# Small TensorE products of a decoder layer's mixing part: one weight shape and whole groups

## The chip, the cores and the metric

The kernel is one program on one core of a Trainium2 chip. The number that counts is the device time of one execution in microseconds (us); the median of three runs is compared. One further execution was recorded by the profiler, and all rows below are read from that one.

Each engine of the core works through its own instructions in order: TensorE (PE) multiplies, VectorE (DVE), ScalarE (ACT) and GpSimd (POOL) do the rest, and SyncE (SP) issues most transfers. An instruction waits for semaphores that other engines raise, and what stands behind it on its engine waits with it.

## What is computed

The reference is one inference step of one layer for 512 prompt positions and 8 samples, in float32. Cut to what matters:

```
x += 0.5 * SwiGLU_1(rms(x))
z  = rms(x) @ w_in                       # one projection, 8448 columns
y_A = RWKV-7 mixing of z's r | k | v | decay | iclr | gate columns
        S = S * decay - (S kk) b^T + v k^T ;  y = S r      # per head, 64 x 64 state
y_B = B * conv3(C * u)
x += (sigmoid(g_A) * y_A + sigmoid(g_B) * y_B) @ w_out
x += 0.5 * SwiGLU_2(rms(x)) ;  x += per-layer embedding ;  final norm
```

The change lies in the mixing part, from `z` to `y_A`.

## The kernel before

All activations stand transposed, 128 features by 520 columns (512 prompt positions and 8 samples), and products run over two halves of 260 columns. A big product of float32 accuracy is made of three passes (high part by high, low by high, high by low), each with 128x128 weights and 260 columns.

In the mixing part (`mix`) two kinds of work share TensorE. The **big products** are the projection's blocks (`product`, lines 792 to 794, 3120 passes in all; `big` in the rows). The **small products** belong to the recurrence. Sixteen heads are handled as eight pairs `p`, two heads on 128 partitions. Time is cut into 16 chunks of 32 positions. For each pair, `stage` prepares decays, keys and masks (its products are `dec`, `icl`, `kn`, `sc`, `bon`), `invert` inverts a triangular 32x32 matrix for each chunk (`ft`), `scan` carries the state through the 16 chunks for two pairs at once (`e` = 0 and 1), and `fin` normalises (`yt`, `gu`).

A chunk of `scan` is made of four groups of four float32 products. In the profile each of these products is two passes, so a group is "x8".

- State product (line 1155, called S below): `AR` by the state S, 64x64 weights, into the bank `xy`, whose rows 0..31 of each head become `u` and whose rows 32..63 become `y`.
- `u` product (line 1160, called W): the inverted matrix by the known rows of `UV`, 32x32 weights. Then two copies on DVE bring `u` into `UV` (line 1163).
- y product of the chunk before (line 1140, called Y): 64 rows by 32 columns of weights, into the other `xy` bank, and then ACT copies y out.
- State update (line 1172, `ds`): 64x64 weights, into the bank `us`. Two DVE operations make the next state (line 1175), one for each pair.

So W and Y use 32 columns of the array's width where S and `ds` use 64.

The functions are generators. A loop at the end of `mix` takes a step of one of them at a time by a planner's clock: a step yields the TensorE time that it is taken to cost and the delay until its generator may go on. That gives the order in which the program is traced. A scheduler then orders the instructions of each engine by readiness in its own model and by that trace order, so that two products of one group can be parted by big ones.

Two PSUM banks (`mw`) serve all small products of `stage`, `invert` and `fin`.

Of the kernel before, what the change touches and what calls it, by code (L numbers as in the profile page):

```python
# [8 lines left out]
F32 = mybir.dt.float32  # L9
# [720 lines left out]
def mix(tc, nc, mp, pp, dp, low0, wprep, mwps, mmps, V, VV, I, O, HS, YM, ysplit, wo_part, ident, pmask):  # L730
# [7 lines left out]
    nc.sync.dma_start(sft, I["sft"])  # L738
    nc.sync.dma_start(cst8, I["cv0"])
    nc.sync.dma_start(smask, I["smask"])  # L740
    nsh = mp.tile([P, NZ, B + 1], F32, name="nsh")
    omm = mp.tile([P, NZ], F32, name="omm")
    hka = mp.tile([P, 4, NT], F32, name="hka")
# [191 lines left out]
    def stage(p):  # L935
# [39 lines left out]

        if p % 2 == 0:
            both[p // 2] = [wide(n, [NC, 2, 64]) for n in ("AR", "UV")]
        ar, uv = both[p // 2]
        AR, UV = ar[:, :, p % 2, :].rearrange("p c (s t) -> p c s t", s=2), uv[:, :, p % 2, :]
        W = wide("W", [NC, 128], 4)  # L980
# [1 line left out]
        v1.tensor_copy(lam, eL[:, :, C])  # L982
        v1.tensor_tensor(AR[:, :, 1, :], c3(r[:, :T]), eL[:, :, 1:], ALU.mult)
        kk = kn
        for cs in GROUPS:
            ps = mwps("kn")
            for g in range(cs.start, cs.stop, GT):
                i = g // GT
                for h, hp in enumerate(HP):
                    nc.tensor.matmul(ps[hp, g - cs.start:g - cs.start + GT], rhs=ident[:GT, :GT], start=True, stop=True,  # L990
                                     lhsT=rs[:GT, 2 * i + h:2 * i + h + 1].broadcast_to([GT, 64]))
            v1.scalar_tensor_tensor(kk[:, cs], k[:, cs], V("k_k", p), ps[:, :cs.stop - cs.start], ALU.mult, ALU.mult)
            yield 0.2 * (cs.stop - cs.start) / GT, 0.5
        v1.scalar_tensor_tensor(AR[:, :, 0, :], c3(kk[:, :T]), -1.0, eL[:, :, 0:C], ALU.mult, ALU.mult)
        yield 0.0, 1.5
        v1.scalar_tensor_tensor(a, a, 1.0, kk, ALU.add, ALU.mult)
# [2 lines left out]
        v1.tensor_tensor(ei, c3(km[:, :T]), ei, ALU.mult)  # L999
        yield 0.0, 1.0  # L1000

        for c0 in range(0, NC, 8):
            ps = mwps("sc")
            for c in range(c0, c0 + 8):
                o = (c - c0) * 64
                for hp in HP:
                    nc.tensor.matmul(ps[hp, o:o + 64], lhsT=fl(BK[hp, c]), rhs=ar[hp, c, p % 2, :], start=True, stop=True)
            v1.tensor_tensor(W[:, c0:c0 + 8, 0:64], ps.rearrange("p (c x) -> p c x", x=64),
                             pmask[:, 0:64].unsqueeze(1).broadcast_to([P, 8, 64]), ALU.mult)
            yield 1.4, 0.6  # L1010

        dm = dp.tile([2, NC, C, CH], F32, tag="dm", name="dm", bufs=2)
        for h in range(2):
# [11 lines left out]
        rk = parts(rk, *t2("rk", N, ("kn", "a")))  # L1025
        yield 0.0, 2.5
        bon = tt("bon", 4)
        for cs in HALF:
            ps = small((blkr,), rk, cs, "bon")
            v1.tensor_tensor(bon[:, cs], vv[:, cs], ps, ALU.mult)  # L1030
            yield 0.25, 0.5
        pool.tensor_copy(bonS[:, p, :], bon[:, T:])

        v3 = c3(vv[:, :T])
# [12 lines left out]
    Nz = mp.tile([P, NC, C], F32, name="Nz")  # L1047
    pool.memset(F4, 0.0)
    pool.memset(Nz, 0.0)
    CH = C // 2  # L1050
    UP = (slice(0, C), slice(64, 64 + C))

# [3 lines left out]
    def invert(p):  # L1056
# [35 lines left out]
        for c0 in range(0, NC, 8):  # L1092
            ps = mwps("ft")
            for i in range(4):
                for odd in range(2):
                    for up in UP:
                        c = c0 + 2 * i + odd
                        qd = slice(up.start + C * odd, up.stop + C * odd)

                        nc.tensor.matmul(ps[qd, i * 128:i * 128 + 96], lhsT=W[up, c, 0:C], rhs=W[up, c, C:],  # L1100
                                         start=i == 0, stop=False, skip_group_check=True)
                        nc.tensor.matmul(ps[qd, i * 128 + 96:(i + 1) * 128], lhsT=Nz[up, c, :], rhs=W[up, c, 0:C],
                                         start=False, stop=False, skip_group_check=True)
            banks.append(ps)
            yield 1.0, 0.8
        for c0, ps in zip(range(0, NC, 8), banks):
            GM = mp.tile([P, 4, 128], F32, tag="Mr", name="GM")
            act.activation(fl(GM), ps, AF.Identity)
# [13 lines left out]

    def scan(q):

        AR, UV = both[q]
        W, lam, _ = zip(st_out[2 * q], st_out[2 * q + 1])
        Y = AR
        S, prev = mp.tile([P, 2, 64], F32, tag="S", name="S", bufs=3), None
        pool.memset(S, 0.0)

        def at(ps, rows, e):
            return ps[rows, 64 * e:64 * e + 64]

        def cols(ps, rows):
            return ps[rows, 0:128].rearrange("p (e x) -> p e x", e=2)

        def y_part(c, xy):
            for e in range(2):
                for hp in HP:
                    nc.tensor.matmul(at(xy, slice(hp.start + C, hp.stop), e), lhsT=W[e][hp, c, C:64],  # L1140
                                     rhs=UV[hp, c, e, :], start=False, stop=True, skip_group_check=True)

        def y_out(c, xy):
            if c % 2 == 0:
# [4 lines left out]

        for c in range(NC):  # L1150
            xy = pp.tile([P, 512], F32, tag="xy", name="xy", bufs=2)
            for e in range(2):

                for hp in HP:
                    nc.tensor.matmul(at(xy, hp, e), lhsT=AR[hp, c, e, :], rhs=S[hp, e, :], start=e == 0, stop=False,  # L1155
                                     skip_group_check=True)
            for e in range(2):
                for h in range(2):
                    up, kp = slice(64 * h, 64 * h + C), slice(64 * h + C, 64 * h + 64)
                    nc.tensor.matmul(at(xy, up, e), lhsT=W[e][kp, c, 0:C], rhs=UV[kp, c, e, :], start=False, stop=True,  # L1160
                                     skip_group_check=True)
            for up in (slice(0, C), slice(64, 64 + C)):
                v1.tensor_copy(UV[up, c], cols(xy, up))
            if c:
                y_part(c - 1, prev)
                y_out(c - 1, prev)
            prev = xy
            yield 0.76, 0.8
            ds = pp.tile([P, 512], F32, tag="us", name="ds")
            for e in range(2):  # L1170
                for hp in HP:
                    nc.tensor.matmul(at(ds, hp, e), lhsT=W[e][hp, c, 64:], rhs=UV[hp, c, e, :], start=True, stop=True)  # L1172
            S1 = mp.tile([P, 2, 64], F32, tag="S", name="S", bufs=3)
            for e in range(2):
                v1.scalar_tensor_tensor(S1[:, e, :], S[:, e, :], lam[e][:, c:c + 1], at(ds, slice(0, P), e),
                                        ALU.mult, ALU.add)
            S = S1
            yield 0.32, 0.8
        y_part(NC - 1, prev)
        y_out(NC - 1, prev)  # L1180
        nc.sync.dma_start(O["wkvp"][2 * q:2 * q + 2].rearrange("q p v -> p q v"), S)
        yield 0.2, 0.5

    def fin(p):
# [30 lines left out]
        act.activation(y1, ps, AF.Identity, scale=V("gn_w", p), bias=V("gn_b", p))  # L1215
        pool.tensor_tensor(y1, y1, bon[:, :T], ALU.add)
        yield 1.4, 2.3
        for j, cs in enumerate(HALF):
            ps = small(gup, sgd, cs, "gu")
            ts = slice(cs.start, min(cs.stop, T))  # L1220
            v1.scalar_tensor_tensor(y1[:, ts], y1[:, ts], 0.5, ps[:, :ts.stop - ts.start], ALU.mult, ALU.mult)
            if j == 1:
                act.activation(gS[:, p, :], ps[:, T - cs.start:], AF.Identity, scale=0.5)
            yield 0.33, 0.5
        y1s[p] = y1

    def sample():
# [239 lines left out]
```

## Time and profile before

| What | Value |
|---|---|
| Median of 3 runs | 1582.39 us (1580.38 to 1582.6) |
| The profiled execution | 1582.78 us, of which the span from the first to the last instruction is 1581.0 us |
| TensorE's mean granted clock | 0.967 of full |
| PE busy | 1513.4 us (96%) |
| DVE, ACT, POOL busy | 1082.8 us (68%), 769.4 us (49%), 396.4 us (25%) |
| Mixing part | from about 406 us to about 1108 us of the span |

Busy shares are averages over stages. A pass of TensorE overlaps the next, so the distance from the start of one row to the start of the next tells its price, and the length of a row does not.

### The profile page before, as it was taken

The page shows a single profiled execution, that of the slowest core. Times are in us where ns is not written, and L with a number is a line of the kernel's source. Part 1 is how long each engine was busy: PE and PEld are TensorE (multiplying, and loading weights), DVE is VectorE, ACT ScalarE, POOL GpSimd, SP SyncE. Part 2 cuts the span into 40 slices and gives each one's busy share as a digit, 9 for nine tenths or more (in the row PEclk, how much of TensorE's full clock was granted, in tenths as well). Part 3 has the DMA queues.
Part 4 walks back from the last instruction along what each step waited for, and adds up shares of the span by engine and source line. Part 5 has one row for each costly group of instructions (what it writes and reads, how often), then busy time and mean ns, then how long its engine had stood idle before and what let it go on. Part 6 is the DMA issues. An engine that isn't in the chain of part 4 may idle for free.

```text
span 1581.0 us, 36116 instructions
## 1 busy us (share of the span) xinstructions
PE 1513.4 (96%) x14772; PEld 1421.5 (90%) x14772; DVE 1082.8 (68%) x2347; ACT 769.4 (49%) x1352; POOL 396.4 (25%) x446
## 2 busy tenths in 40 slices
PE   8899999999999999999999999999989999999996
PEld 7799999998899988888888787799988999999996
DVE  8876666655797776568778357765688656666566
ACT  7655555555544424424442253143465555555543
POOL 0333433342322120111212004211004343434401
PEclk9899999999999999999999599899999999999998
DMA  5678888885332211212221122224336787888723
GB/s 179 160 164 183 181 179 185 177 202 137 98 85 79 84 38 53 65 43 65 75 71 44 37 74 77 88 78 149 96 93 168 177 182 182 180 187 177 168 60 112
DMA packets 116133, 191.08 MB, mean 121 GB/s; under 512 B 41800, under 2 KB 51016, under 8 KB 115968
## 3 DMA queue, kind: packets, MB, share of 16 engines
q1 hardware_dynamic: 92352, 138.44, 28.2%
q0 software_dynamic: 23616, 50.34, 19.8%
q8 instruction: 116, 1.90, 0.5%
q14 instruction: 49, 0.40, 0.1%
HBM read 177.73 MB, written 10.74 MB: 119 GB/s over the span
## 4 chain that ended last, share of the span: by engine, by line
PE 47%; DVE 8%; ACT 1%; DMA 1%; issue 1%; SPq 0%; DVEq 0%; ACTq 0%
PE big L171 9%; PE big L173 8%; PE big L172 8%; PE big L792 5%; PE big L794 4%; PE big L793 4%; PE ds L1172 2%; PE xy L1155 1%; DVE lo L132 1%; PE xy L1140 1%; PE xy L1160 1%; DVE raw L166 0%; DMA sdr<-stg 0%; DVE ft L1079 0%; DVE F L1081 0%
## 5 line engine op out<-in xcount | busy, mean ns | idle before, releaser
L130 ACT ACTIVATE hi<-raw 128x512 fp32r<-128x512 f32 (+2 forms) x427 | 318.4, 749 | 316.1 <-PE big L172 166.9
L792 PE MATMUL big<-xh,hi 128*128 128x260 f32 x1040 | 317.3, 305 | 0.4 <-DVE cc L862 0.2
L793 PE MATMUL big<-xl,hi 128*128 128x260 f32 x1040 | 306.2, 295 | 0.0
L794 PE MATMUL big<-xh,lo 128*128 128x260 f32 x1040 | 305.6, 294 | 0.5 <-DVE lo L132 0.5
L132 DVE TENSOR_TENSOR lo<-raw,hi 128x512 fp32r<-128x512 f32 (+2 forms) x263 | 239.2, 912 | 61.7 <-ACT hi L130 57.2
L792 PEld LDWEIGHTS big<-xh,hi 128*128 128x128 f32 x1040 | 202.2, 194 | 14.0 <-issue 0.5
L793 PEld LDWEIGHTS big<-xl,hi 128*128 128x128 f32 x1040 | 202.6, 195 | 5.3 <-issue 0.7
L171 PE MATMUL big<-hh,hi 128*128 128x260 f32 x704 | 203.5, 289 | 3.9 <-DVE x L470 3.9
L794 PEld LDWEIGHTS big<-xh,lo 128*128 128x128 f32 x1040 | 202.0, 194 | 5.4 <-DVE lo L132 0.8
L173 PE MATMUL big<-hh,lo 128*128 128x260 f32 x704 | 199.5, 283 | 0.0
L172 PE MATMUL big<-hl,hi 128*128 128x260 f32 x704 | 199.4, 283 | 0.0
L171 PE MATMUL big<-th,hi 128*128 128x260 f32 x640 | 182.8, 286 | 9.2 <-ACT th L319 5.3
L172 PE MATMUL big<-tl,hi 128*128 128x260 f32 x640 | 182.3, 285 | 3.6 <-DVE tl L320 3.6
L173 PE MATMUL big<-th,lo 128*128 128x260 f32 x640 | 181.2, 283 | 0.0
L171 PEld LDWEIGHTS big<-hh,hi 128*128 128x128 f32 x704 | 133.2, 189 | 7.7 <-DVE x L470 4.3
L470 DVE SCALAR_TENSOR_TENSOR x<-big,x 128x260 f32<-128x260 f32 x176 | 74.7, 426 | 94.8 <-PE big L173 94.8
L172 PEld LDWEIGHTS big<-hl,hi 128*128 128x128 f32 x704 | 133.3, 189 | 0.0
L173 PEld LDWEIGHTS big<-hh,lo 128*128 128x128 f32 x704 | 133.3, 189 | 0.0
L171 PEld LDWEIGHTS big<-th,hi 128*128 128x128 f32 x640 | 121.3, 190 | 11.0 <-ACT th L319 6.0
L172 PEld LDWEIGHTS big<-tl,hi 128*128 128x128 f32 x640 | 121.1, 189 | 4.9 <-DVE tl L320 4.9
L171 PE MATMUL big<-xh,hi 128*128 128x260 f32 x400 | 115.2, 292 | 7.9 <-ACT hi L130 5.4
L166 DVE TENSOR_TENSOR raw<-raw 128x512 f32<-128x512 f32 x160 | 114.0, 713 | 11.0 <-DMA raw<-in_wu 5.6
(306 smaller groups left out, 3488.2 us busy)
## 6 DMA issues: line engine op xcount, KB each, us to landing
raw<-in_win SPq DMA_DIRECT2D x66, 512.0 KB, 3.8
raw<-in_wd SPq DMA_DIRECT2D x80, 256.0 KB, 2.9
lo<-in_wd POOLq DMA_DIRECT2D x72, 256.0 KB, 4.6
raw<-in_wu SPq DMA_DIRECT2D x24, 512.0 KB, 3.7
raw<-in_wg SPq DMA_DIRECT2D x23, 512.0 KB, 4.4
raw<-in_wg SPq DMA_DIRECT2D x40, 256.0 KB, 3.5
raw<-in_wu SPq DMA_DIRECT2D x40, 256.0 KB, 3.7
lo<-in_wg POOLq DMA_DIRECT2D x18, 512.0 KB, 5.5
```

Source lines behind the costliest of these rows:

```text
L130: nc.scalar.activation(self.hi[:, ks], self.raw[:, ks], AF.Identity)
L132: self.eng.tensor_tensor(self.lo[:, ks], self.raw[:, ks], self.hi[:, ks].bitcast(F32), ALU.subtract)
L166: nc.vector.tensor_tensor(self.raw, a.raw, b.raw, ALU.add)
L171: nc.tensor.matmul(ps[:, :HN], lhsT=hi, rhs=x[0], start=first, stop=False, skip_group_check=True)
L172: nc.tensor.matmul(ps[:, :HN], lhsT=hi, rhs=x[1], start=False, stop=False, skip_group_check=True)
L173: nc.tensor.matmul(ps[:, :HN], lhsT=lo, rhs=x[0], start=False, stop=last, skip_group_check=True)
L470: nc.vector.scalar_tensor_tensor(X[m][:, cs], ps, 0.5, X[m][:, cs], ALU.mult, ALU.add)
L792: nc.tensor.matmul(ps[:, :HN], lhsT=hi[:, k, :], rhs=hh[k][:, cs], start=k == 0, stop=False)
L793: nc.tensor.matmul(ps[:, :HN], lhsT=hi[:, k, :], rhs=hl[k][:, cs], start=False, stop=False)
L794: nc.tensor.matmul(ps[:, :HN], lhsT=lo[:, k, :], rhs=hh[k][:, cs], start=False, stop=k == nk - 1)
L1140: nc.tensor.matmul(at(xy, slice(hp.start + C, hp.stop), e), lhsT=W[e][hp, c, C:64], rhs=UV[hp, c, e, :], start=False, stop=True, skip_grou ...
L1172: nc.tensor.matmul(at(ds, hp, e), lhsT=W[e][hp, c, 64:], rhs=UV[hp, c, e, :], start=True, stop=True)
```

## The change

It has four parts.

1. The scan's four groups all get 64x64 weights. W takes all 64 rows and columns of its block, and so does Y. For this the rows of `UV` that will hold `u` must be zero at first: a block of zeros (`zd`) in DRAM is made from `Nz`, and two transfers for each pair of pairs put it into `UV`. The known rows now enter `y` twice, in W and in Y, so their mask is halved once (`pmask`).
2. The y product of chunk c is traced straight after the state update of chunk c, no longer after the `u` product of chunk c+1. The steps' planned costs become 0.55 and 0.6 us (0.76 and 0.32).
3. `behind` puts an ordering edge from each product of a group to the group's first, and the product whose operand is made last is traced first.
4. In `kn`, `sc`, `bon`, `gu` and `ft` the products of both halves are traced in one step before what consumes them.

```diff
+    for h in range(2):
+        v1.tensor_scalar(pmask[64 * h + C:64 * h + 64, C:64], pmask[64 * h + C:64 * h + 64, C:64], 0.5, None, ALU.mult)
...
             both[p // 2] = [wide(n, [NC, 2, 64]) for n in ("AR", "UV")]
+            for up in UP:
+                nc.sync.dma_start(both[p // 2][1][up].rearrange("p c e v -> p (c e v)"), zd)
...
-        for c0 in range(0, NC, 8):
-            ps = mwps("sc")
+        sps = [mwps("sc") for _ in range(2)]
+        for c0, ps in zip(range(0, NC, 8), sps):
             for c in range(c0, c0 + 8):
                 o = (c - c0) * 64
                 for hp in HP:
                     nc.tensor.matmul(ps[hp, o:o + 64], lhsT=fl(BK[hp, c]), rhs=ar[hp, c, p % 2, :], start=True, stop=True)
+        for c0, ps in zip(range(0, NC, 8), sps):
             v1.tensor_tensor(W[:, c0:c0 + 8, 0:64], ps.rearrange("p (c x) -> p c x", x=64),
                              pmask[:, 0:64].unsqueeze(1).broadcast_to([P, 8, 64]), ALU.mult)
-            yield 1.4, 0.6
+        yield 2.8, 1.2
...
+    zd = dp.tile([C, NC * 128], F32, name="zd")
+    for i in range(NC * 128 // 512):
+        nc.sync.dma_start(zd[:, i * 512:(i + 1) * 512], Nz[0:C].rearrange("p c j -> p (c j)"))
...
+        def behind(group):
+            for x in group[1:]:
+                tc.add_manual_dep(x.ins, group[0].ins.name, mybir.DependencyInfo(
+                    mybir.DependencyClass.NoSync, mybir.DependencyReason.DATA), reason="order")
...
         def y_part(c, xy):
-            for e in range(2):
-                for hp in HP:
-                    nc.tensor.matmul(at(xy, slice(hp.start + C, hp.stop), e), lhsT=W[e][hp, c, C:64],
-                                     rhs=UV[hp, c, e, :], start=False, stop=True, skip_group_check=True)
+
+            return [nc.tensor.matmul(at(xy, hp, e), lhsT=W[e][hp, c, 0:64], rhs=UV[hp, c, e, :], start=False, stop=True,
+                                     skip_group_check=True) for e in range(2) for hp in HP]
...
+            group = []
+            for e in (1, 0):
+
+                for hp in HP:
+                    group.append(nc.tensor.matmul(at(xy, hp, e), lhsT=AR[hp, c, e, :], rhs=S[hp, e, :], start=e == 1,
+                                                  stop=False, skip_group_check=True))
+            behind(group)
             for e in range(2):
 
                 for hp in HP:
-                    nc.tensor.matmul(at(xy, hp, e), lhsT=AR[hp, c, e, :], rhs=S[hp, e, :], start=e == 0, stop=False,
-                                     skip_group_check=True)
-            for e in range(2):
-                for h in range(2):
-                    up, kp = slice(64 * h, 64 * h + C), slice(64 * h + C, 64 * h + 64)
-                    nc.tensor.matmul(at(xy, up, e), lhsT=W[e][kp, c, 0:C], rhs=UV[kp, c, e, :], start=False, stop=True,
+                    nc.tensor.matmul(at(xy, hp, e), lhsT=W[e][hp, c, 0:64], rhs=UV[hp, c, e, :], start=False, stop=True,
                                      skip_group_check=True)
             for up in (slice(0, C), slice(64, 64 + C)):
                 v1.tensor_copy(UV[up, c], cols(xy, up))
-            if c:
-                y_part(c - 1, prev)
-                y_out(c - 1, prev)
-            prev = xy
-            yield 0.76, 0.8
+            yield 0.55, 0.8
             ds = pp.tile([P, 512], F32, tag="us", name="ds")
+            group = []
             for e in range(2):
-                for hp in HP:
-                    nc.tensor.matmul(at(ds, hp, e), lhsT=W[e][hp, c, 64:], rhs=UV[hp, c, e, :], start=True, stop=True)
+                for hp in HP[::-1]:
+                    group.append(nc.tensor.matmul(at(ds, hp, e), lhsT=W[e][hp, c, 64:], rhs=UV[hp, c, e, :],
+                                                  start=True, stop=True))
+            behind(group + y_part(c, xy))
             S1 = mp.tile([P, 2, 64], F32, tag="S", name="S", bufs=3)
...
             S = S1
-            yield 0.32, 0.8
-        y_part(NC - 1, prev)
-        y_out(NC - 1, prev)
+            y_out(c, xy)
+            yield 0.6, 0.8
```

What the scheduler makes of it is shown by TensorE's order. The rows name the line, the operation and what it writes and reads; `x4` is four products in a row. First the tenth chunk of the second scan, on TensorE, before: its state update, the y product of the chunk before it, and between them big passes.

```order
L1172 MATMUL ds<-UV,W 64x64
L792 MATMUL big<-xh_4972,hi 128x260
L793 MATMUL big<-xl_4973,hi 128x260
L1172 MATMUL ds<-UV,W 64x64 x3
L794 MATMUL big<-xh_4972,lo 128x260
L1140 MATMUL xy<-UV,W 32x64 x4
```

The same chunk in the changed program.

```order
L795 MATMUL big<-xh_4972,hi 128x260
L1186 MATMUL ds<-UV,W 64x64 x4
L1154 MATMUL xy<-UV,W 64x64 x4
L796 MATMUL big<-xl_4973,hi 128x260
L797 MATMUL big<-xh_4972,lo 128x260
```

Three leaves of the big stream became one, and eight products of one shape stand side by side. Next, a little later on TensorE, the state and `u` products of the eleventh chunk, before.

```order
L792 MATMUL big<-xh_4976,hi 128x260
L1155 MATMUL xy<-S,AR 64x64 x2
L793 MATMUL big<-xl_4977,hi 128x260
L1155 MATMUL xy<-S,AR 64x64 x2
L1160 MATMUL xy<-UV,W 32x64 x4
L794 MATMUL big<-xh_4976,lo 128x260
```

And in the changed program.

```order
L797 MATMUL big<-xh_4974,lo 128x260
L1171 MATMUL xy<-S,AR 64x64 x4
L1177 MATMUL xy<-UV,W 64x64 x4
L795 MATMUL big<-xh_4976,hi 128x260
L796 MATMUL big<-xl_4977,hi 128x260
```

The parted state product is whole, and the `u` product has its shape. The third place is SP's queue where the buffer `UV` of the first scan is taken over for the third. Before, with the semaphores that each transfer waits for:

```order
L1065 DMA Mr<-dm 32x512 [waits DMAHW5_49]
L120 DMA raw<-in_win 128x1024 [waits DMAHW6_49,DVE_49]
L1181 DMA out_wkvp<-S 128x2x64 [waits DMAHW7_49,DVE_49]
L120 DMA raw<-in_win 128x1024 [waits DMAHW0_49,DVE_49]
L932 DMA wdi<-in_wdi 128x128 [waits DMAHW1_49,Pool_49]
```

And in the changed program.

```order
L1074 DMA Mr<-dm 32x512 [waits DMAHW5_49]
L120 DMA raw<-in_win 128x1024 [waits DVE_49]
L982 DMA UV<-zd 32x2048 [waits DMAHW7_49,DVE_49,PE_49]
L1196 DMA out_wkvp<-S 128x2x64 [waits DMAHW0_49,DVE_49]
L982 DMA UV<-zd 32x2048 [waits DMAHW1_49]
L120 DMA raw<-in_win 128x1024 [waits DMAHW2_49,DVE_49]
```

The two transfers of zeros stand beside the store of the finished state, ahead of the same weight block as that store did.

## Rows read from the trace of the kernel before

**Rows 1.** First line of the profile's page.

```profile
span 1581.0 us, 36116 instructions
```

**Rows 2.** Stretches: us; busy us of PE, PEld, DVE, ACT, POOL; clock; DMA; GB/s.

```profile
400.00:1120.00 720.00, 693.08 (x8148) 611.65 (x8148) 506.78 (x1289) 277.79 (x567) 132.48 (x199) 0.95 0.25 73
740.00:860.00 120.00, 112.17 (x1452) 101.13 (x1452) 94.98 (x254) 49.31 (x101) 24.81 (x39) 0.96 0.24 66
```

**Rows 3.** TensorE's waits, 400 to 1120 us: total us, times, longest.

```profile
PE kn L990 <- DVE rs L54: 5.8, 3, 3.1
...
PE yt L1213 <- ACT stg L1236: 0.2, 1, 0.2
```

**Rows 4.** TensorE in order of time, groups left whole: start us, length us, what.

```profile
688.83 0.28 PE L794 MATMUL big<-xh,lo 128*128 128x260 f32 x1
689.04 0.45 PE L1172 MATMUL ds<-UV,W 64*64 64x64 f32 x8
689.42 0.39 PE L792 MATMUL big<-xh,hi 128*128 128x260 f32 x1
689.64 0.28 PE L793 MATMUL big<-xl,hi 128*128 128x260 f32 x1
689.76 0.28 PE L794 MATMUL big<-xh,lo 128*128 128x260 f32 x1
...
690.48 0.28 PE L794 MATMUL big<-xh,lo 128*128 128x260 f32 x1
690.69 0.45 PE L1155 MATMUL xy<-S,AR 64*64 64x64 f32 x8
691.07 0.41 PE L1160 MATMUL xy<-UV,W 32*32 32x64 f32 x8
691.41 0.41 PE L1140 MATMUL xy<-UV,W 64*32 64x64 f32 x8
691.76 0.39 PE L792 MATMUL big<-xh,hi 128*128 128x260 f32 x1
691.98 0.28 PE L793 MATMUL big<-xl,hi 128*128 128x260 f32 x1
```

**Rows 5.** TensorE in order of time, a run of one shape.

```profile
705.47 1.15 PE L1007 MATMUL sc<-AR,BK 64*64 64x64 f32 x32
706.45 0.40 PE L1155 MATMUL xy<-S,AR 64*64 64x64 f32 x8
```

**Rows 6.** TensorE in order of time, a state product that is parted.

```profile
851.53 0.33 PE L1155 MATMUL xy<-S,AR 64*64 64x64 f32 x4
851.79 0.39 PE L793 MATMUL big<-xl,hi 128*128 128x260 f32 x1
852.11 0.33 PE L1155 MATMUL xy<-S,AR 64*64 64x64 f32 x4
852.38 0.41 PE L1160 MATMUL xy<-UV,W 32*32 32x64 f32 x8
```

**Rows 7.** Weight loads by line: ns minimum, median, maximum; first and last start.

```profile
L1172 PEld LDWEIGHTS ds<-UV,W x512: 129/133/228, 543.2 to 1044.1; 64*64 64x64 f32 x171
L1160 PEld LDWEIGHTS xy<-UV,W x512: 101/105/172, 541.6 to 1041.5; 32*32 32x32 f32 x171
```

**Rows 8.** DVE in order of time, beside the chunk of rows 4.

```profile
687.55 0.60 DVE L1163 COPY UV<-xy 32x128 f32<-32x128 f32 x2 [0.22 <-PE xy L1160]
689.63 0.47 DVE L1175 SCALAR_TENSOR_TENSOR S<-S,lam,ds 128x64 f32<-128x64 f32 x2
```

**Rows 9.** Transfers of weight blocks: count, KB each, median us to landing.

```profile
raw<-in_win SPq DMA_DIRECT2D x66, 512.0 KB, 3.8
```

**Rows 10.** A stretch at the lower clock (columns as in rows 2).

```profile
871.00:915.30 44.30, 44.30 (x447) 34.84 (x446) 15.30 (x38) 10.02 (x22) 1.05 (x3) 0.50 0.18 42
```

**Rows 11.** TensorE in order of time inside that stretch.

```profile
875.79 0.64 PE L1140 MATMUL xy<-UV,W 64*32 64x64 f32 x8
876.36 0.58 PE L794 MATMUL big<-xh,lo 128*128 128x260 f32 x1
876.74 0.42 PE L792 MATMUL big<-xh,hi 128*128 128x260 f32 x1
```

More of the change, by code (lines that the diff above doesn't have):

```diff
@@ L984, in stage @@
         kk = kn
-        for cs in GROUPS:
-            ps = mwps("kn")
+        kps = [mwps("kn") for _ in GROUPS]
+        for cs, ps in zip(GROUPS, kps):
             for g in range(cs.start, cs.stop, GT):
@@ L991, in stage @@
                                      lhsT=rs[:GT, 2 * i + h:2 * i + h + 1].broadcast_to([GT, 64]))
+        for cs, ps in zip(GROUPS, kps):
             v1.scalar_tensor_tensor(kk[:, cs], k[:, cs], V("k_k", p), ps[:, :cs.stop - cs.start], ALU.mult, ALU.mult)
-            yield 0.2 * (cs.stop - cs.start) / GT, 0.5
+        yield 1.0, 1.0
         v1.scalar_tensor_tensor(AR[:, :, 0, :], c3(kk[:, :T]), -1.0, eL[:, :, 0:C], ALU.mult, ALU.mult)
@@ L1027, in stage @@
         bon = tt("bon", 4)
-        for cs in HALF:
-            ps = small((blkr,), rk, cs, "bon")
+        for cs, ps in [(cs, small((blkr,), rk, cs, "bon")) for cs in HALF]:
             v1.tensor_tensor(bon[:, cs], vv[:, cs], ps, ALU.mult)
-            yield 0.25, 0.5
+        yield 0.5, 1.0
         pool.tensor_copy(bonS[:, p, :], bon[:, T:])
@@ L1104, in invert @@
             banks.append(ps)
-            yield 1.0, 0.8
+        yield 2.0, 0.8
         for c0, ps in zip(range(0, NC, 8), banks):
@@ L1127, in scan @@
         Y = AR
-        S, prev = mp.tile([P, 2, 64], F32, tag="S", name="S", bufs=3), None
+        S = mp.tile([P, 2, 64], F32, tag="S", name="S", bufs=3)
         pool.memset(S, 0.0)
@@ L1217, in fin @@
         yield 1.4, 2.3
-        for j, cs in enumerate(HALF):
-            ps = small(gup, sgd, cs, "gu")
+        for j, (cs, ps) in enumerate([(cs, small(gup, sgd, cs, "gu")) for cs in HALF]):
             ts = slice(cs.start, min(cs.stop, T))
@@ L1223, in fin @@
                 act.activation(gS[:, p, :], ps[:, T - cs.start:], AF.Identity, scale=0.5)
-            yield 0.33, 0.5
+        yield 0.66, 1.0
         y1s[p] = y1
```

## The prediction, made before the changed kernel ran

> **What bounds the kernel now.** I read the page first, then the mixing part alone, then what TensorE waits for there, and last its rows in order of time, for prices. The span is 1581.0 us [rows 1]; the profiled execution took 1582.78 us, 0.4 us over the median of three, so a sum made against it holds for the median as well. From 400 to 1120 us TensorE is busy for 693 of 720 us and DVE for 507 [rows 2]. A busy PE can still be waiting, so the waits decide: over that stretch they come to some 26 us in 22 rows, from 5.8 us down to 0.2 us [rows 3]. The other 95% of the mixing part is the time in which TensorE takes in its stream. What shortens the stream shortens the kernel, as long as the others keep up.
>
> The stream has a price that busy time hides. Two big passes follow each other in 0.12 us. When a group of small products stands between them, the last big pass is followed after 0.21 us, the group holds TensorE, and the first big pass behind it is followed after 0.22 us [rows 4]. A whole `ds` group takes 0.81 us from one big pass to the second one behind it (688.83 to 689.64), so it adds 0.81 - 0.24 = 0.57 us to the big stream. The visit with S, W and Y takes 1.50 us (690.48 to 691.98) and adds 1.26 us; in it S takes 0.38, W 0.34 and Y 0.35 us, nearly as much as a group with the entry from big passes. So each change of shape is paid for, not only the one from 128x128. A chunk that is nowhere parted costs 1.83 us.
>
> Inside one shape a product is cheap: sixteen `sc` products with 64x64 weights take 0.98 us (705.47 to 706.45), 0.06 us each, and the state product that follows in the same shape starts as if it belonged to them [rows 5].
>
> **The change part by part.** *One shape, y beside the state.* Both visits of a chunk become eight products of one shape: 0.57 + 4 x 0.06 = 0.81 us each, 1.62 for the chunk. That is 0.21 us less, over 64 chunks 13.4 us.
>
> *Whole groups.* A state product parted by one big pass takes 0.85 us (851.53 to 852.38) [rows 6], where the whole group and a big pass take 0.38 + 0.12; parting costs 0.35 us. From TensorE's order I counted how often the big stream is left for a product of the scan: 198 times before (87 for S, 91 for `ds`, 20 for Y), 115 times in the changed program (57, 57, and one for W). All 64 `ds` groups and all 64 S groups stand whole; before, 35 and 38 were parted. Of the 83 leaves saved, 20 are a Y that stood alone: entry, group and return come to 0.21 + 0.35 + 0.22 - 0.24 = 0.54 us against 0.35 beside another group, 0.19 each, 3.8 us. The other 63 at 0.35 give 22.0 us.
>
> *Halves together.* `kn`, `sc` and `ft` leave the big stream 36 times in place of 47. At some 0.3 us each, between the two prices above, 3.3 us. `bon` and `gu` have the big products' shape; for them it is nothing.
>
> The stream thus gets 13.4 + 25.8 + 3.3 = 42.5 us shorter at the full clock.
>
> *What it adds.* The W and Y weights are twice as wide. The load of 64 columns takes 133 ns, that of 32 takes 105 [rows 7]. Yet the groups differ by 0.03 us for eight passes (`ds` 0.38, Y 0.35 in [rows 4]), so the loads run ahead, and the sum above, made with 64-column groups, holds this already. If every load's 28 ns were on the path, it would be 64 x 16 x 28 ns = 29 us; that is the upper bound and a rival below. The Trainium skill, "TensorE: Matmul & The Clock Gate", section "LDWEIGHTS (loading the stationary operand)", lets the load's time grow with the number of columns and speaks against the wider weights; the loads' own lengths agree with it, the distance between passes does not.
>
> The four transfers into `zd` and the first two into `UV` stand in SP's queue near the first weight blocks of the mixing part, and the later ones wait for the earlier. A block takes 3.8 us to land [rows 9], so the first blocks may come one landing late: 0 to 4 us. I take 1, because a block is read only after the one before it, whose 48 passes of 0.12 us hold TensorE for 5.8 us. The later zeros stand beside the store of the state that waits for the same scan's end, so the block behind them waits no longer than before. The two operations on the mask are shorter than a copy of 0.3 us [rows 8] and lie among DVE's first ones of the part, when TensorE has big products: nothing, 0.6 us without that cover.
>
> *Waits.* The y group waits for the copies of `u`, as `ds` ahead of it does: no new wait. ACT's copy of y moves with it; behind it in ACT's queue stand splits of weights and evacuations, which wait on the y product as long as they do now. What loses cover is the way from W to `ds`: Y no longer runs under the two copies of 0.60 us, and the way from `ds` to the next S has to hold the two state operations of 0.47 us [rows 8]. In the order, the median of big passes between W and `ds` goes from 8 to 9 and between `ds` and S from 8 to 7; without any stand 4 and 3 chunks before, 0 and 5 after. Seven passes and a change of shape are over 1.2 us, so the cover stays. Since the stream runs 6% faster against the same DVE work, I put 1.5 us of new waits on it; the bounds are 0 and the DVE rival below.
>
> Sum: 1582.8 - 42.5 + 1 + 1.5 = 1543 us.
>
> **The rivals.** *The clock stays up.* From 871 to 915 us the granted clock is 0.5 of full, its 1.2 GHz level, although TensorE never idles [rows 10]: a Y group takes 0.57 us there for 0.35, a big pass after it 0.38 for 0.22 [rows 4, 11], so 44.3 us hold some 27 us of work. Ahead of the fall stood two runs of `sc` and scan groups with next to no big passes. If the denser stream does not fall there, 17 us more are gained, and a few in shorter stretches: 1523 us. For it: fewer small visits for the same big passes. Against it: the changed order has the same crowd, 7 + 25 `sc` products with four scan groups between and behind.
>
> *DVE takes half of it back.* From 740 to 860 us DVE is busy for 95 of 120 us [rows 2]; with 6% less time that is 84%, and its operations of a pair's preparation stand in one queue with the copies that the scan waits for. If half of the saving turns into waits for `UV`, S and the two `mw` banks, which now are both asked for at once: 1543 + 21 = 1564 us. Against it: waits are 26 us now at 79% as well as at lower shares.
>
> *The weight loads are on the path*, 29 us: 1572 us. The wide `ds` group speaks against it. The section of the Trainium skill named above would lead there.
>
> *Slower, by the clock.* `sc` now comes as 32 products at once, some 2 us, and with scan groups beside them nearly 3 us without a big pass. The stretch before the fall at 871 us looked like that. If such crowds bring the clock down in more scans, each further 44 us stretch costs 17 us; two and a half of them eat the whole saving, and three more give 1543 + 51 = 1594 us. Against it: at 705 us two such runs stand beside scan groups [rows 5] and the clock stayed up, and the number of such places within scans does not grow.
>
> *The change not doing what it says* is not open: the order shows whole groups of one shape.
>
> **How the numbers follow.** The forecast, the stream's saving with waits and clock about as now, gets 0.62 and 1530 to 1556 us; the clock that stays up 0.13 (1515 to 1530); DVE 0.13 (1556 to 1575); the loads 0.03 (about 1572); more of the lower clock 0.09, of which about half ends slower than before and the rest spreads from 1560 to 1586. Leaving out 1 in 10 or so at either end gives 1520 to 1570 us. A difference under 0.2%, 3.2 us, is about what cannot be told from none here: 1579 to 1586 gets 0.04 from two further stretches of low clock or DVE waits that eat all. Slower gets 0.06, faster 0.90 by these cases; since they price what is seen and not what is missed, I move 0.03: 0.87, 0.05 and 0.08.
>
> **What would show it.** Right: from a state product, x16 in one row, to the second big pass behind it some 0.8 us, the same for `ds`; no `ds` x2 with x6 apart; big passes as dear as now; TensorE's waits in the mixing part still near 26 us; the scans some 10 us shorter each. Wrong: rows of waits for `UV` or S (lines 1163 and 1175 before) that grow to 10 us or more; eight products of one shape that take well over 0.62 us; or a clock row that falls for longer than 44 us.

## The result, and the profile after

The changed kernel takes 1517.69 us (median of 4 runs, 1516.04 to 1518.29); the kernel before takes 1581.78 us beside it (4 runs, 1580.38 to 1582.6). The ratio is 0.9594, with a 95% interval of 0.9577 to 0.9611. The forecast was 1543 us and its range ended at 1520 us: the direction was right, and the gain of 64 us is over half as much again as the 39 us forecast.

The page of the changed kernel: span, busy time and instructions by engine, and the granted clock in 40 slices.

```profile
span 1516.5 us, 36191 instructions
...
PE 1446.9 (95%) x14772; PEld 1390.4 (92%) x14772; DVE 1076.5 (71%) x2349; ACT 770.1 (51%) x1352; POOL 398.5 (26%) x447
...
PEclk9899999999998999999999999999999999999998
```

The clock row of the kernel before:

```profile
PEclk9899999999999999999999599899999999999998
```

The span is 64.5 us shorter than in [rows 1]. The clock row has no deep dip left; in the kernel before, slice 23 stood at 5, and that is the stretch of [rows 10]. All four executions of the changed kernel were granted 0.977 to 0.980 of the clock on average, where the profiled one of the kernel before was granted 0.967, so the dip is not missing from the profiled one alone.

Stretches of the changed kernel (columns as in [rows 2]): the mixing part, and a stretch as long as that of [rows 10], mostly of the third scan, which ends at 873 us.

```profile
400.00:1044.00 644.00, 616.92 (x8089) 571.13 (x8088) 492.99 (x1273) 272.71 (x556) 134.62 (x199) 0.98 0.29 83
836.00:880.30 44.30, 42.54 (x704) 37.56 (x705) 31.35 (x93) 17.37 (x37) 8.17 (x11) 0.96 0.30 76
```

The mixing part now ends near 1044 us, 64 us earlier, so it holds nearly the whole gain. In these 44.3 us TensorE takes 704 instructions where [rows 10] has 447.

What TensorE waits for, 400 to 1044 us (total us, times, longest):

```profile
PE kn L995 <- DVE rs L54: 5.2, 2, 2.7
PE dec L923 <- ACT sg L946: 3.4, 2, 2.8
PE xy L1171 <- DVE S L1191: 2.3, 5, 0.9
...
PE ds L1186 <- DVE UV L1180: 1.5, 3, 1.0
```

All rows together come to 26.6 us. Those of [rows 3] come to 26.1 us, but 3.4 us of these lie behind the mixing part, so it waits some 3 to 4 us longer than before. The waits for `UV` and S, where DVE could have taken time back, are 1.5 and 2.3 us. In the kernel before they were 4.3 and 0.5 us:

```profile
PE ds L1172 <- DVE UV L1163: 4.3, 6, 1.6
...
PE xy L1155 <- DVE S L1175: 0.5, 1, 0.5
```

TensorE in order of time, one visit with S and W and one with `ds` and Y, to set beside [rows 4] (start, length, what):

```profile
826.91 0.28 PE L795 MATMUL big<-xh,hi 128*128 128x260 f32 x1
827.12 0.45 PE L1171 MATMUL xy<-S,AR 64*64 64x64 f32 x8
827.40 0.40 PE L1177 MATMUL xy<-UV,W 64*64 64x64 f32 x8
827.74 0.39 PE L796 MATMUL big<-xl,hi 128*128 128x260 f32 x1
827.96 0.28 PE L797 MATMUL big<-xh,lo 128*128 128x260 f32 x1
...
833.28 0.28 PE L797 MATMUL big<-xh,lo 128*128 128x260 f32 x1
833.50 0.45 PE L1186 MATMUL ds<-UV,W 64*64 64x64 f32 x8
833.78 0.40 PE L1154 MATMUL xy<-UV,W 64*64 64x64 f32 x8
834.11 0.39 PE L795 MATMUL big<-xh,hi 128*128 128x260 f32 x1
834.33 0.28 PE L796 MATMUL big<-xl,hi 128*128 128x260 f32 x1
```

From the last big pass to the second one behind, each visit takes 1.05 us, and two big passes alone would take 0.24: the visit adds 0.81 us, which is the price predicted. These two are typical: the medians of 46 such visits with S and W and of 44 with `ds` and Y are 1.05 us too.

To see where 64.5 us came from, I split the mixing part of each trace, from the first big pass to the last pass of the output projection. Each pair of neighbouring passes has a price: the median distance of such a pair of shapes at the full clock and without a wait. The sum of these prices is the stream. What a pair takes beyond its price is a wait if TensorE idled there, and the clock's if the granted clock was 0.5 there. The three add up to the mixing part, because what is left over is counted in one of them. This is an accounting, good to some 2 us.

| Kernel (profiled execution) | Mixing part, us | Stream | Waits | Clock | us at clock 0.5 |
|---|---|---|---|---|---|
| before | 701.8 | 644.3 | 28.1 | 29.4 | 71.7 |
| changed | 638.2 | 596.0 | 31.0 | 11.2 | 27.3 |
| difference | -63.6 | -48.3 | +2.9 | -18.2 | -44.4 |

The last column says it plainly: both kernels spend some 27 us at 0.5 in short stretches, and what the changed kernel no longer has is the one stretch of 44.3 us.

### The profile page after: what moved, and what is told of

Same layout as the page of the kernel before. It is cut to its first block, busy times and chain, and to the rows that moved or that the text cites. A ratio compares the mean times of both kernels' runs of the same rounds, so it can differ in the third digit from the quotient of the medians.

```text
span 1516.5 us, 36191 instructions
## 1 busy us (share of the span) xinstructions
PE 1446.9 (95%) x14772; PEld 1390.4 (92%) x14772; DVE 1076.5 (71%) x2349; ACT 770.1 (51%) x1352; POOL 398.5 (26%) x447
## 4 chain that ended last, share of the span: by engine, by line
PE 75%; DVE 15%; ACT 3%; issue 3%; DMA 2%; POOL 1%; SPq 0%; DVEq 0%; ACTq 0%; POOLq 0%
PE big L171 16%; PE big L173 16%; PE big L172 16%; PE big L795 6%; PE big L796 6%; PE big L797 5%; DVE lo L132 2%; PE xy L1171 1%; PE ds L1186 1%; PE xy L1177 1%; ACT hi L130 1%; PE ft L1123 1%; PE xy L1154 1%; DVE F L1090 1%; ACT W L1127 1%
## 5 line engine op out<-in xcount | busy, mean ns | idle before, releaser
L795 PE MATMUL big<-xh,hi 128*128 128x260 f32 x1040 | 310.5, 299 | 1.7 <-ACT cc L847 1.0
L797 PE MATMUL big<-xh,lo 128*128 128x260 f32 x1040 | 299.6, 289 | 2.0 <-DVE lo L132 2.0
L796 PE MATMUL big<-xl,hi 128*128 128x260 f32 x1040 | 300.8, 289 | 0.0
L171 PE MATMUL big<-xh,hi 128*128 128x260 f32 x400 | 114.9, 291 | 8.4 <-ACT hi L130 5.5
L166 DVE TENSOR_TENSOR raw<-raw 128x512 f32<-128x512 f32 x160 | 113.9, 713 | 12.6 <-DMA raw<-in_wu 5.6
```

Source lines behind the costliest of these rows:

```text
L166: nc.vector.tensor_tensor(self.raw, a.raw, b.raw, ALU.add)
L171: nc.tensor.matmul(ps[:, :HN], lhsT=hi, rhs=x[0], start=first, stop=False, skip_group_check=True)
L795: nc.tensor.matmul(ps[:, :HN], lhsT=hi[:, k, :], rhs=hh[k][:, cs], start=k == 0, stop=False)
L796: nc.tensor.matmul(ps[:, :HN], lhsT=hi[:, k, :], rhs=hl[k][:, cs], start=False, stop=False)
L797: nc.tensor.matmul(ps[:, :HN], lhsT=lo[:, k, :], rhs=hh[k][:, cs], start=False, stop=k == nk - 1)
```

## The experiments

The theory to test: the stream is about 48 us shorter, by parts whose prices add up, and the other 18 us are the low stretch of the third scan, which is gone. Rivals: one part alone brings the gain; the wider weights cost something that the other parts hide; the low stretch belongs to one of the parts (narrow shapes, or parted groups), or to crowds of small products.

**Each part undone.** `free_order` takes the edges and the last-made-first order away, so groups can be parted again:

```diff
-            for x in group[1:]:
+            for x in []:
...
-            for e in (1, 0):
+            for e in range(2):
```

> The changed kernel without the ordering edges and with its products traced in the old order (pair 0 first, head 0 first), so that big passes part the groups again: TensorE's order leaves the big stream for state and ds products 165 times, where the changed kernel does 115 times; shapes and the place of y stay. Theory (the stream of TensorE sets the time, and parted groups are what keeps the clock low once it fell): 50 leaves at 0.35 us cost 17 us, 1535 us, and with a long stretch at the lower clock inside a scan some 1550 us. Rival (grouping is worth little, the 64 us come from shape and place): 1518 to 1523 us.

`narrow` brings back the old shapes of W and Y, the full mask, and no zeros:

```diff
-                    nc.tensor.matmul(at(xy, hp, e), lhsT=W[e][hp, c, 0:64], rhs=UV[hp, c, e, :], start=False, stop=True,
+                    nc.tensor.matmul(at(xy, up, e), lhsT=W[e][kp, c, 0:C], rhs=UV[kp, c, e, :], start=False, stop=True,
```

> The changed kernel with the old shapes: 32x32 weights for u, 64x32 for y, no zeros, no halved mask; groups whole, y beside ds. 147 changes from one small shape to another in place of 15. Theory: 132 changes at 0.11 us more than going on in one shape, some 14.5 us: 1532 us, with waits and the clock as in the changed kernel. Rival (wider weights cost as much in their loads as the shape saves): 1515 to 1520 us.

`halves_apart` traces each half's products and their consumer in a step of its own again (`kn`, `sc`, `bon`, `gu`, `ft`):

```diff
-        sps = [mwps("sc") for _ in range(2)]
-        for c0, ps in zip(range(0, NC, 8), sps):
+        for c0 in range(0, NC, 8):
+            ps = mwps("sc")
```

> The changed kernel with kn, sc, ft, bon and gu traced half by half as before: 171 leaves of the big stream in place of 159. Theory: 12 leaves at 0.3 to 0.35 us, 4 us: 1522 us. Rival (holding both PSUM banks at once costs waits that the halves apart don't have): below 1516 us.

`y_late` traces the y product behind the next chunk's `u` product again:

```diff
+            if c:
+                y_part(c - 1, prev)
+                y_out(c - 1, prev)
...
-            behind(group + y_part(c, xy))
+            behind(group)
```

> The changed kernel with the y product of chunk c traced behind the u product of chunk c+1, as before, in the 64x64 shape and with the old planned costs of the two steps. 178 leaves of the big stream in place of 159, 23 of them a y product that stands alone. Theory: a y product alone costs 0.54 us where it costs 0.23 beside ds, 23 x 0.31 = 7 us: 1525 us. Rival (the place of y matters through the bank that it holds and ACT's copy, not through TensorE): 1517 to 1519 us, with other waits.

| Kernel | Median us (range) | Ratio to before (95%) | Stream | Waits | Clock | Stream above the changed kernel's |
|---|---|---|---|---|---|---|
| free_order | 1536.39 (1531.85 to 1540.5) | 0.9729 (0.9664 to 0.9795) | 617.0 | 28.3 | 13.3 | 21.0 |
| narrow | 1543.14 (1535.2 to 1546.41) | 0.9765 (0.9697 to 0.9834) | 612.4 | 33.7 | 10.5 | 16.4 |
| halves_apart | 1520.55 (1518.78 to 1524.13) | 0.9633 (0.9572 to 0.9694) | 600.8 | 28.7 | 11.5 | 4.8 |
| y_late | 1527.12 (1526.8 to 1531.78) | 0.9681 (0.9607 to 0.9755) | 602.7 | 31.4 | 11.4 | 6.7 |

Undone one at a time, the four parts cost 48.9 us of stream, against the 48.3 of the whole change, and none has the whole gain. Between single kernels the times are less sharp: the intervals of `halves_apart` and `y_late` overlap that of the changed kernel (0.9577 to 0.9611), so their small prices rest on the traces. The median of `narrow` is 11 us above the 1532 us expected. Its profiled execution was its fastest, and its three others are 6 to 11 us longer; two of these were granted 0.974 of the clock where the profiled one was granted 0.980, and the third, at 0.980, is not explained.

In `free_order`, TensorE in order of time:

```profile
836.50 0.28 PE L797 MATMUL big<-xh,lo 128*128 128x260 f32 x1
836.71 0.33 PE L1186 MATMUL ds<-UV,W 64*64 64x64 f32 x2
836.96 0.38 PE L795 MATMUL big<-xh,hi 128*128 128x260 f32 x1
837.28 0.38 PE L1186 MATMUL ds<-UV,W 64*64 64x64 f32 x5
```

A `ds` group is parted again: from the first piece's start to the second's it takes 0.57 us, for 0.12 of a big pass and 0.06 of one small product, which is the x2; the other 0.39 us are a little above the 0.35 that parting was priced at. (The sixth pass of the second piece stands in a row further on, between passes of Y.) In `narrow`, the visit with `ds` and Y, and the one with S and W:

```profile
816.32 0.28 PE L795 MATMUL big<-xh,lo 128*128 128x260 f32 x1
816.53 0.45 PE L1180 MATMUL ds<-UV,W 64*64 64x64 f32 x8
816.91 0.41 PE L1147 MATMUL xy<-UV,W 64*32 64x64 f32 x8
817.25 0.39 PE L793 MATMUL big<-xh,hi 128*128 128x260 f32 x1
817.47 0.28 PE L794 MATMUL big<-xl,hi 128*128 128x260 f32 x1
...
828.25 0.28 PE L794 MATMUL big<-xl,hi 128*128 128x260 f32 x1
828.46 0.45 PE L1165 MATMUL xy<-S,AR 64*64 64x64 f32 x8
828.84 0.41 PE L1171 MATMUL xy<-UV,W 32*32 32x64 f32 x8
829.18 0.39 PE L795 MATMUL big<-xh,lo 128*128 128x260 f32 x1
829.41 0.28 PE L793 MATMUL big<-xh,hi 128*128 128x260 f32 x1
```

They take 1.15 and 1.16 us where the changed kernel's take 1.05, although half of their weights are narrower: the first group is followed after 0.38 us when the shape changes behind it, and after 0.28 when not. In `y_late`, a y product that stands alone:

```profile
840.33 0.28 PE L797 MATMUL big<-xh,lo 128*128 128x260 f32 x1
840.54 0.45 PE L1154 MATMUL xy<-UV,W 64*64 64x64 f32 x8
840.92 0.39 PE L795 MATMUL big<-xh,hi 128*128 128x260 f32 x1
841.14 0.28 PE L796 MATMUL big<-xl,hi 128*128 128x260 f32 x1
```

0.81 - 0.24 = 0.57 us, where beside `ds` it adds 0.81 - 0.57 = 0.24. The order of `y_late` has 23 that stand alone: 23 x 0.33 = 7.6 us, near the 6.7 found.

The low stretch came back in none of the four: the longest time at 0.5 is 13.7 us in one piece, and 27 to 31 us in all. So no one part has to be in its new form for the stretch to be gone.

**Two parts alone, and crowds.** The other side: one part put into the old form. `edges_only` has the groups whole and nothing else, `wide_only` the wide shapes and nothing else. `sc_twice` is the changed kernel with each `sc` product done twice, which doubles the crowd of small products that stood ahead of the fall at 871 us:

```diff
-                for hp in HP:
+                for hp in HP * 2:
```

`before_again` is the kernel before with two empty lines, to learn whether the long stretch comes back each time.

> The old kernel with only the groups made whole: the ordering edges, and the product whose operand is made last traced first. Shapes, the place of y and the halves as before. TensorE's order leaves the big stream 186 times in place of 253. Theory: about 25 us of stream less, 1557 us where the long stretch at the lower clock stays and some 1540 us where it goes. Rival (grouping is worth little without one shape): above 1570 us.

> The old kernel with only the 64x64 weights for u and y, the zeros and the halved mask. 17 changes between small shapes in place of 135, and 204 leaves of the big stream in place of 253, since the scheduler's order moves with it. Theory: 118 changes of shape at 0.11 us and 49 leaves at 0.35 us, some 30 us: 1552 us with the long stretch at the lower clock, 1535 us without. Rival (weight loads of 64 columns on the path, 28 ns each): above 1570 us.

> The changed kernel with each sc product made twice into the same place, so that its runs in one shape are 64 products long; TensorE's order is otherwise the same. Tests whether a crowd of small products brings the granted clock down. Theory of the price alone: 256 products at 0.058 us, 15 us, 1532 us, with the lower clock for about as long as now (27 us of the mixing part). If crowds bring the clock down: stretches at 0.5 behind the three crowds inside scans, 1545 us or more.

> The kernel of before once more, with nothing changed but two empty lines, for a second profile and more times. Theory (18 us of the change's gain are a stretch of 44 us at the lower clock inside the second half of the third scan, which not every execution of the old kernel has): executions near 1582 us, whose profile shows a long stretch of that kind, and now and then one near 1565 us without it; the stream of TensorE is the same in both, 644 us of the mixing part. Rival (the old kernel's times differ by its waits, not by the clock): a profile in which some other execution time goes with other waits.

| Kernel | Median us (range) | Ratio to before (95%) | Stream | Waits | Clock | us at 0.5 |
|---|---|---|---|---|---|---|
| edges_only | 1552.96 (1551.39 to 1554.89) | 0.9793 (0.9773 to 0.9813) | 617.6 | 35.5 | 19.3 | 51.2 |
| wide_only | 1537.66 (1534.83 to 1538.55) | 0.9693 (0.9673 to 0.9713) | 615.1 | 30.1 | 9.5 | 23.9 |
| sc_twice | 1529.81 (1528.52 to 1531.87) | 0.9648 (0.9628 to 0.9667) | 610.4 | 28.3 | 8.7 | 20.5 |
| before_again | 1584.52 (1582.55 to 1594.13) | 1.0009 (0.9991 to 1.0028) | 644.4 | 28.5 | 31.1 | 75.1 |

The stretch in `before_again` (columns as in [rows 2]):

```profile
874.50:915.50 41.00, 41.00 (x425) 32.40 (x426) 14.18 (x34) 9.89 (x22) 0.85 (x2) 0.50 0.18 41
```

It belongs to the old program, at the same place. `edges_only` also falls in its third scan, but for 10.2 us, and in its first and fourth scans for 13.7 and 17.1 us, so whole groups by themselves do not keep the clock up; `wide_only` does not fall in its third scan, and its longest stretch, in the fourth, is 13.7 us. The stretches of `edges_only` (columns as in [rows 2]):

```profile
876.70:886.90 10.20, 10.20 (x133) 7.81 (x117) 2.97 (x9) 4.57 (x10) 0.00 (x0) 0.50 0.03 6
948.40:965.50 17.10, 11.88 (x103) 9.49 (x99) 13.96 (x27) 1.56 (x5) 8.07 (x8) 0.50 0.25 78
```

Put into the old kernel alone, the groups save 26.7 us of stream and the shapes 29.2 us, near the 25 and 30 us expected. Together that is more than the 48.3 us of all four parts, since the scheduler's order moves with each of them: with the wide shapes alone, 30 groups of S and `ds` are parted in the trace where some 70 were. So the price of a part depends on which others stand beside it, and the wide shapes alone already bring the old kernel to 1537.66 us, with the long stretch gone.

Twice the crowd costs 14.4 us of stream and brings no clock down: behind each of the three crowds that stand inside scans, `sc_twice` keeps the full clock for 37 us or more. Its clock row, whose mixing part is slices 11 to 28:

```profile
PEclk9899999999999999999999999999989999999998
```

In the changed kernel a crowd of small products is thereby out as a cause by itself.

**What the low stretch needs.** Ahead of the fall TensorE's rows of the kernel before are these (in brackets what it waited for):

```profile
865.99 1.15 PE L1007 MATMUL sc<-AR,BK 64*64 64x64 f32 x32
867.38 0.76 PE L1172 MATMUL ds<-UV,W 64*64 64x64 f32 x8 [0.24 <-DVE UV L1163]
...
870.40 0.39 PE L920 MATMUL bon<-rkh,blkr 128*128 128x260 f32 x1 [1.12 <-DVE W L1008]
```

A crowd, and then a wait of 1.12 us at `bon`. `old_sc_spread` moves that place in the kernel before, by a longer planned delay behind `sc` for the last pair alone; in its trace `bon` is gone from there, and some of the `sc` products, which were to stay, moved too. `bon_close` does the reverse in the changed kernel: `bon` is traced close behind `sc`. And `lull_old` and `lull_changed` put 60 products of two columns (result unused) into the second scan of either kernel, to bring the clock down there and see when each form of the scan gets it back.

```diff
-            yield 1.4, 0.6
+            yield 1.4, 3.0 if p == NT - 1 else 0.6
...
-        yield 2.8, 1.2
+        yield 2.8, 0.0 if p == NT - 1 else 1.2
...
-        yield 0.0, 2.5
+        yield 0.0, 0.0 if p == NT - 1 else 2.5
...
+            if q == 1 and c == 8:
+                low = mwps("lull")
+                for _ in range(60):
+                    nc.tensor.matmul(low[:GT, 0:2], lhsT=blkr.bitcast(F32)[:, 0:GT], rhs=heads, start=True, stop=True)
```

> The old kernel with a longer planned delay behind the last pair's two sc steps (3.0 in place of 0.6), which moves that pair's bon products away from the place just ahead of the fall of the clock at 871 us, and with them TensorE's wait of 1.1 us for their bank; the sc products and the scan groups around them stay. If that wait beside the crowd brought the clock down: no long stretch at 0.5 in the third scan, 1566 us. If the crowd or the form of the scan does it: the long stretch stays, 1583 us.

> The old kernel with the same 60 products ahead of the ninth chunk of the second scan, where its own profile shows the full clock. Theory (parted groups and changes of shape keep the clock down once it fell): at 0.5 to the end of the second scan, some 35 us, 1584 + 5.5 + 14 = 1604 us. Rival (the clock comes back as in the changed kernel, and the long stretch of the third scan has a cause of its own there): 1592 us.

> The changed kernel with 60 products of two columns (128x104 weights, as the first kn product has) put ahead of the ninth chunk's state product in the second scan; their result is not used. They hold TensorE for 60 x 0.092 = 5.5 us with next to no columns, to bring the clock down in the middle of a scan. Theory (the stream of whole groups lets the clock come back soon): at most some 10 us at 0.5 behind the lull, 1525 us. Rival (a scan at the lower clock keeps it, whatever its shape): at 0.5 to the scan's end, some 30 us, 1535 us or more.

> The changed kernel with the last pair's bon products planned right behind its sc products, as they stand in the old kernel ahead of the fall of the clock at 871 us; TensorE's order up to there is the same, and the stream is as long. If the wait of bon for the sc bank beside the crowd brings the clock down in any form of the scan, and it then stays: a stretch of some 40 us at 0.5 behind the sc products, 1517.7 + 17 = 1535 us. If it falls but whole groups bring it back: a stretch of 3 to 10 us there, 1520 us. If it doesn't fall: 1518 us.

| Kernel | Median us (range) | Ratio to before (95%) | Stream | Waits | Clock | us at 0.5 |
|---|---|---|---|---|---|---|
| old_sc_spread | 1572.13 (1570.99 to 1576.29) | 0.9934 (0.991 to 0.9957) | 646.2 | 29.4 | 12.6 | 30.7 |
| lull_old | 1606.27 (1586.6 to 1613.6) | 1.0087 (1.0042 to 1.0132) | 655.1 | 28.7 | 44.1 | 105.8 |
| lull_changed | 1535.31 (1533.72 to 1540.74) | 0.9693 (0.9671 to 0.9715) | 606.7 | 30.0 | 22.2 | 51.2 |
| bon_close | 1515.33 (1511.69 to 1517.15) | 0.9576 (0.9545 to 0.9606) | 594.9 | 31.0 | 9.1 | 20.5 |

`old_sc_spread`, the same 44.3 us as in [rows 10]:

```profile
871.00:915.30 44.30, 44.30 (x630) 36.98 (x630) 29.80 (x91) 17.97 (x37) 3.98 (x9) 1.00 0.25 65
```

With a few instructions of one pair moved, the old form keeps its clock there and does 630 passes for 447. Part of these are other work, since the scan now ends at 905 us; the third scan takes 74.9 us, from its first state product to its last state update, where it took 93.6. The clock's loss falls from 29.4 to 12.6 us, 16.8 less, while the median falls by about 10; stream and waits are 3.2 us longer. All four executions were granted 0.974 to 0.977. So narrow and parted groups do not bring the long stretch by themselves: a small change of the order ahead of 871 us removes it. This is what was expected if the wait beside the crowd brought the clock down, but as `sc` moved too, it does not single out that wait.

`bon_close`, mostly the third scan, which ends at 871 us:

```profile
836.00:880.00 44.00, 42.54 (x735) 37.55 (x734) 34.20 (x106) 19.50 (x41) 6.57 (x10) 1.00 0.28 68
```

The changed kernel does not fall when `bon` stands close behind the crowd, with a wait of 0.89 us for S there. The edit did not make the old place again, so it does not settle what triggers the fall, and the wait at `bon` stays a candidate. Its ratio is not to be told from the changed kernel's.

`lull_old`: from where the clock falls to where it returns, the rest of the second scan, and the third scan's stretch.

```profile
696.40:720.30 23.90, 23.90 (x161) 21.61 (x160) 4.45 (x10) 2.26 (x5) 1.84 (x2) 0.50 0.04 8
720.40:749.00 28.60, 28.60 (x371) 23.29 (x371) 19.67 (x48) 7.21 (x16) 4.17 (x8) 1.00 0.17 44
894.40:938.80 44.40, 44.40 (x447) 34.94 (x448) 15.35 (x38) 10.02 (x22) 1.05 (x3) 0.50 0.18 40
```

`lull_changed`: the same two stretches of its second scan.

```profile
681.60:698.70 17.10, 17.10 (x117) 16.62 (x116) 0.66 (x3) 1.45 (x2) 0.00 (x0) 0.50 0.00 1
698.80:727.00 28.20, 28.12 (x418) 25.39 (x418) 25.81 (x62) 7.72 (x17) 6.50 (x11) 1.00 0.25 60
```

The lulls were three times as long as planned (16.7 us for 5.5): each product is two passes, and most of these ran at 0.5. Behind their ends, at 709.7 and 694.0 us, the clock came back after 10.6 us in the old form and 4.7 us in the new one, both in the middle of a scan. So the old form does not hold a low clock to the scan's end by itself. Whether 10.6 against 4.7 is the form or the place is open, with one look at each. The times alone would have misled: 1606 us fits the theory's 1604 for `lull_old`, and 1535 us the rival's for `lull_changed`, but both hold a lull 11 us longer than planned.

Three of the nine runs of `lull_old` ended at 1586.6 to 1587.9 us, some 20 us below the rest, and were granted 0.972 or 0.973 of the clock where the rest were granted 0.952 to 0.958. Of the 47 executions of the kernel before beside these experiments, two took 1565.07 and 1567.6 us and were granted 0.978, where the other 45 were granted 0.959 to 0.968. From 0.966 to 0.978 over 1580 us is, as an estimate, some 38 us less at 0.5. That is near the long stretch, so the old program seems to escape it now and then, in the same order of instructions. Where those runs kept their clock is not known, since none was profiled. If it was there, the order ahead of the fall makes the long stretch likely, but does not decide it alone.

## Why the prediction missed

**One shape**: 13.4 us predicted, 16.4 found. The visits cost what was predicted, 0.81 us each, and 1.15 + 1.16 us in `narrow` are 0.21 more per chunk, as predicted. The other 3.0 us were not placed.

**Whole groups**: 22.0 predicted, 21.0 found, but not for the same count: the prediction has 63 leaves at 0.35 us, and `free_order` 50 leaves more than the changed kernel, 0.42 us each. That the totals agree so well is in part luck.

**Y alone**: 3.8 predicted, 6.7 found. The step set a lone Y, 0.54, against 0.35 beside another group; that was the price beside a group of another shape. In one shape it is 0.24. `y_late` also has 23 such products, the kernel before 20.

**Halves together**: 3.3 predicted, 4.8 found. The 0.3 us a leave was a choice between two prices, and low: `halves_apart` leaves the big stream 12 times more, at 0.40 us each.

**Waits and zeros**: 2.5 predicted, 2.9 found; the zeros' 1 us was not measured apart. That DVE takes half of the saving back is refuted: its share over the mixing part rose from 70% (498.9 of 708 us) to 77%, and the waits for `UV` and S stayed small.

**Weight loads**: the rival of 29 us is refuted, since the wide forms are faster by 16.4 us with all their loads. The Trainium skill, "TensorE: Matmul & The Clock Gate", section "LDWEIGHTS (loading the stationary operand)", lets a load take longer by its columns, and the loads' lengths agree, 28 ns more for 32 more columns [rows 7]; here no cost of it showed in the time.

**The step that failed** is the likeliest case's "waits and clock about as now". The low stretch of [rows 10] is gone: 18.2 us. That was the rival "the clock stays up", put at 0.13, with the same crowd in the changed order as the argument against it. The crowd was the wrong sign to read: twice the crowd left the clock up, and the old form without the changed parts kept it when a few instructions of one pair were moved. A stretch that a small change of order removes should not have been carried into a program whose order is new throughout; its going away deserved the larger chance. Nothing in the change aimed at it, so these 18.2 us are luck. Without them the time would have been about 1536 us, inside the 1530 to 1556 us of the likeliest case: what the change was made for was priced nearly right.

The sum with what was measured, which closes because the accounting does: 1542.8 - 5.8 (stream 48.3 for 42.5) + 0.4 (waits) - 18.2 (clock) - 0.9 (outside the mixing part, 64.5 against 63.6) = 1518.3 us, the profiled execution's time. Of the miss of 25 us, three quarters is the clock.

Still open is what makes the clock fall at 871 us and what keeps it down for 44 us. Shown is that the narrow shapes, the parting and longer crowds of `sc`, each put alone into the changed kernel, do not bring the long stretch (`narrow`, `free_order`, `sc_twice`), and that the old form can be without it too (`old_sc_spread`).

## What to carry to other kernels

Price a small product by the distance from the last big pass to the second one behind it, once for each shape and neighbour: on a busy TensorE, leaving the stream and changing shape can cost more than doubling the weights' width does, and such prices add up over the program. A part's price depends on the order in which the scheduler puts the rest, so undo it in the new program and also try it alone in the old one. Where the profile has a long stretch at the low clock that a whole new order passes through, give its loss and its return separate cases, and do not assume that it stays. To keep a group whole, see which operand is made last, trace that product first and put ordering edges from the others to it; the two were tried only together here.

## What was not expected of the hardware

TensorE stayed at 0.5 of its clock (1.2 GHz) for 44 us without idling at all in the records (44.30 of 44.30 us busy), and the same kernel with one pair's products moved spent the same stretch at 1.00, equally busy. Busy time in the records therefore does not tell whether the clock will be granted.

Changing between two small shapes costs about 0.10 us more than going on in one (0.38 against 0.28 us behind a group with 64x64 weights), and it does so for 64x64 to 32x32 and to 64x32 alike (`narrow`).
